# Output product of a gated-merge decoder block: seven half-size products instead of eight, with sums on GpSimd

## The chip, the cores and the metric

The kernel runs on one core of one Trainium2 chip. The time is that of one execution on the device, in microseconds. Three executions of the kernel before took 1394.12, 1395.01 and 1397.86 us; the median is 1395.01. One more execution was recorded by the hardware profiler and is the source of the profile.

A core has five engines with instruction streams of their own: TensorE (PE in the profile; its weight loads are PEld), VectorE (DVE), ScalarE (ACT), GpSimd (POOL) and SyncE (SP), which here only issues DMAs. They meet at semaphores.

## The reference

One layer of a decoder trunk on x of 1024 tokens by 1024 channels, all in float32. A modulated RMS norm gives `h`; `h @ w_in` feeds a gMLP mixer (`y_a`) and a Mamba-2 SSD mixer (`y_b`); two gates merge them; an output product, a residual and a last norm follow:

```python
merged = jax.nn.sigmoid(g_a) * (y_a @ w_proj_a) + jax.nn.sigmoid(g_b) * (y_b @ w_proj_b)
x = x + gate[:, None, :] * (merged @ w_out)
...
return rms_norm(x, final_norm_w)
```

The change concerns `merged @ w_out`, a product of 1024x1024 by 1024x1024, and what surrounds it.

## The kernel before

**Precision.** Every float32 operand of a big product is split in two: a high part (an ACT copy into the type float32r) and a low part (DVE subtracts the high part from the original). A product is then three matmuls: high by high, high by low, low by high.

**Seven products.** The big products before the output product already go by Winograd's variant of Strassen: both operands are cut in quarters, and seven products p1 to p7 of sums of quarters take the place of eight. With quarters a11, a12, a21, a22 and b11 to b22 they are p1 = a11 b11, p2 = a12 b21, p3 = s4 b22, p4 = a22 t4, p5 = s1 t1, p6 = s2 t2, p7 = s3 t3, with sums s1 = a21 + a22, s2 = s1 - a11, s3 = a11 - a21, s4 = a12 - s2 on one side and t1 to t4 on the other.

**Stages.** First come the products of `h` with `w_in` (pairs of column blocks, `pair`, lines 718 to 774), their convolutions and gates (`conv_done` and its neighbours, from 1007). They share six buffers of 128x1024, handed out by `wide` (176). `later` (506) puts off a function by a number of slots, one slot per product of 12 matmuls; `gate_part2` (909) puts off eight calls of `gated_weights` (919), each of which loads 128 rows of `w_out`, multiplies them on POOL by the gate row and stores them. Weights of the merge are prepared there too (`wb_quarter`, 948). Then follow the SSD chunks, with the product for `y_a` between them, and then the branch product `y_b @ w_proj_b` as seven products in the order p1, p2, p5, p3, p6, p7, p4 (1612), eight units of 12 matmuls each; `ahead` (1727) loads seven units ahead and makes operands four units ahead. As a quarter of the branch product is complete, `merged` (1711) adds the other branch to it under its gate and splits the sum in high and low parts. The quarters come in the order (channels 0 to 511, tokens 0 to 511), (channels 0 to 511, tokens 512 to 1023), (channels 512 to 1023, tokens 512 to 1023), and last (channels 512 to 1023, tokens 0 to 511), which are a11, a21, a22 and a12 of the output product.

**The output product** (1835 to 1926) is a plain one. `wo_load` and `wo_parts` bring and split the gated weights, in part during the last branch products. The first two row tiles are multiplied together, k by k; then six row tiles of 128 tokens follow, each 2 halves x 8 k x 3 matmuls of 128x512 (`out_product`, 1868). Behind each row tile DVE adds x, ACT squares and sums, DVE takes the inverse root in nine small operations (`inv_root`, 1857), DVE multiplies by root and norm weight, and the row leaves by SP. The last row is cut in pieces of 512, 256 and 256 columns.

**Order.** Matmuls and loads (line 100) keep the order in which the program has them (`pin`). From the last gate pair to the end of the branch product, `hand[0]` (44 to 58, 1447, 1836) does the same for DVE, ACT and POOL; elsewhere a scheduler may put their instructions in another order when the program is built. SP issues all loads and ACT the stores, each in order: a load that waits for its buffer holds the loads behind it. Buffers of 128x512 are handed out from the list `room` by `slot_tile` (1577) and returned by `give`, the longest free first.

Of the kernel before, what the change touches and what calls it, by code (L numbers as in the profile page):

```python
# [35 lines left out]
def hybrid_kernel(  # L36
# [30 lines left out]
    def dt_(shape, name):  # L67
        return dram.tile(shape, F32, name=name, tag=name)
# [8 lines left out]
    wo_d = [dt_([P, D], f"wo_d{k}") for k in range(KT)]  # L77
# [26 lines left out]
    def store(dst, src):  # L104
        A.dma_start(dst, src)
# [400 lines left out]
    def later(delay, f, *a):  # L506
        tasks.append((slot[0] + delay, f, a))
# [401 lines left out]
    def gate_part2(gb):  # L909
        for n in range(2):  # L910
            pg = bank(f"pg{n}")
            ns = slice(n * 512, (n + 1) * 512)
            mm(pg, ones, gacc[0][:, ns])
            V.tensor_add(gb[:, ns], pg, gb[:, ns])
        V.tensor_scalar_mul(gb, gb, 0.5)
        for k in range(KT):
            later(7 + 11 * k, gated_weights, gb, k)

    def gated_weights(gb, k):

        w = wide(f"wog{k}")
        load(w, w_out[k * P : (k + 1) * P, :])
        G.tensor_mul(w, w, gb)  # L923
        store(wo_d[k], w)


    WB = {"p5": 0, "p7": 1, "p6": 2, "p3": 3, "p4": 4}
# [763 lines left out]
            load(ma, mt_d[b][:, hs])  # L1691
        gates[b, h] = th, ma

    mhl = {}
    places = []

    def m_slot(name):
        if m_sl:
            if not places:
                pool, b = m_sl.pop(0)  # L1700
                t = pool.tile([P, 3, 512], F32R, name=f"m{name}", tag="sl", bufs=b)
                places.extend(t[:, i] for i in range(3))
            return places.pop(0)
        return places.pop(0) if places else slot_tile(name, F32R)

    m_sl = [(p2r, 2), (p2q, 3), (p2q, 3), (p2q, 3), (p2r, 2)]


    GATES = {"p5": (0, 0), "p6": (0, 1), "p7": (4, 1), "p4": (4, 0)}

    def merged(b, h, c, name):

        th, ma = gates.pop((b, h))
        V.scalar_tensor_tensor(th, th, 1.0, c, op0=ALU.add, op1=ALU.mult)
        V.tensor_add(th, th, ma)
# [5 lines left out]
        A.copy(hi, th)  # L1721
        V.tensor_sub(lo, th, f32(hi))
        mhl[b, h] = hi, lo

    LEAD, LOAD = 4, 7

# [38 lines left out]
    wo, wor = {}, {}  # L1765
    KO = (4, 5, 6, 7, 0, 1, 2, 3)

    def wo_load(k):
        wor[k] = [[slot_tile(f"wo{v}{k}_{c}", F32R) for v in "hl"] for c in range(2)]
        for c in range(2):  # L1770
            load(f32(wor[k][c][1]), wo_d[k][:, c * 512 : (c + 1) * 512])

    def wo_parts(k):
        for hi, lo in wor[k]:
            A.copy(hi, f32(lo))
            V.tensor_sub(lo, f32(lo), f32(hi))
        wo[k] = wor.pop(k)

    at_unit = {}
    for i, g in enumerate(groups[NG - 2:]):  # L1780
# [26 lines left out]
    for u, (nm, k) in enumerate(units):  # L1807
        if k == 0:
            if nm == "p1":
                psy = banks("yp2", "y")  # L1810
                psx = banks("x", "x")
            elif nm == "p5":
                psy = banks(f"y{nm}", "y")
            elif nm == "p6":
                room.extend(rb_r[0])
            ps = psy if nm in ("p2", "p5", "p3") else psx
        multiply(u, ps)
        for f in at_unit.get(u, ()):
# [7 lines left out]
        if nm in ("p7", "p4") and k % 2 == 0:  # L1826
            n = k // 2 + (4 if nm == "p4" else 0)
            due_m = 2 * (16 - len(mhl)) - len(places) - 3 * len(m_sl)
            if len(room) >= 4 + due_m and len(wor) + len(wo) < KT:
                wo_load(KO[len(wor) + len(wo)])  # L1830
        if nm == "p4" and k % 2 and wor:
            wo_parts(next(iter(wor)))
# [5 lines left out]
    for n in KO:  # L1838
        if n not in wo:
            if n not in wor:  # L1840
                wo_load(n)
            wo_parts(n)
    ps3.__exit__(None, None, None)


    ps4 = ctx.enter_context(tc.tile_pool(name="ps4", bufs=1, space=PSUM, reuse_waits="tile"))

    for n in range(4):
        ps4.tile([P, 512], F32, name=f"one{n}_0", tag="one", bufs=4)

    def pj_tile(name):
        return ps4.tile([P, 1024], F32, name=name, tag="pj", bufs=2)

    def one(name):
        return ps4.tile([P, 512], F32, name=name, tag="one", bufs=4)

    def inv_root(sq):

        y, t, v = sq[:, 2:3], sq[:, 3:4], sq[:, 1:2]
        V.tensor_scalar(t, sq[:, 0:1], 1.0 / D, EPS, op0=ALU.mult, op1=ALU.add)  # L1860
        V.tensor_scalar(y.bitcast(I32), t.bitcast(I32), -0.5, float(0x5F3759DF), op0=ALU.mult, op1=ALU.add)
        V.tensor_scalar_mul(v, t, -0.5)
# [3 lines left out]
        return y  # L1866

    def out_product(ps, t, k, c, cs):

        tsl = slice(t % 4 * P, (t % 4 + 1) * P)  # L1870
        for a, b in ((0, 0), (0, 1), (1, 0)):
            mm(ps, mhl[k, t // 4][a][:, tsl], wo[k][c][b][:, cs], k == KO[0] and a + b == 0, k == KO[-1] and a == 1)

    xrs = {}

    def ask_x(t):
        xrs[t] = p2q.tile([P, S], F32, name=f"xr{t}", tag="dcy", bufs=3)
        load(xrs[t], x[t * P : (t + 1) * P, :])

    tiles = [4, 5, 6, 7, 0, 1, 2, 3]  # L1880
    ask_x(4)
    ask_x(5)
    fnw = p2r.tile([P, D], F32, name="fnw", tag="w4", bufs=4)
    load(fnw, final_norm_w.unsqueeze(0).to_broadcast([P, D]))
    pws = {t: pj_tile(f"po{t}") for t in tiles[:2]}
    for k in KO:
        for t in tiles[:2]:
            for h in range(2):
                out_product(pws[t][:, h * 512 : (h + 1) * 512], t, k, h, slice(0, 512))

    for n, t in enumerate(tiles):
        tsl = slice(t * P, (t + 1) * P)
        xr = xrs.pop(t)
        if n + 2 < NCH:
            ask_x(tiles[n + 2])
        r = p2r.tile([P, S], F32, name=f"r{t}", tag="dcy", bufs=2)
        sq = dthq[:, 4 * n : 4 * n + 4]
        last = n == NCH - 1
        if last:
            py = [one(f"po{t}_{h}") for h in range(3)]  # L1900
            pieces = [(py[0], 0, 512), (py[1][:, 0:256], 512, 256), (py[2][:, 0:256], 768, 256)]
            part = dde[:, 0:4]
        else:
            pw = pws[t] if n < 2 else pj_tile(f"po{t}")
            pieces = [(pw[:, h * 512 : (h + 1) * 512], h * 512, 512) for h in range(2)]
        for m, (ps, c0, w) in enumerate(pieces):
            cs = slice(c0, c0 + w)
            for k in KO if n > 1 else ():
                out_product(ps, t, k, c0 // 512, slice(c0 % 512, c0 % 512 + w))
            if last:  # L1910
                V.tensor_add(r[:, cs], ps, xr[:, cs])
                A.activation(xr[:, cs], r[:, cs], AF.Square, accum_out=part[:, m : m + 1])  # L1912
                G.tensor_mul(r[:, cs], r[:, cs], fnw[:, cs])  # L1913
        if last:
            V.scalar_tensor_tensor(sq[:, 0:1], part[:, 0:1], part[:, 1:2], part[:, 2:3], op0=ALU.add, op1=ALU.add)
            y = inv_root(sq)
            V.tensor_scalar_mul(r[:, 0:512], r[:, 0:512], y)
            nc.sync.dma_start(out[tsl, 0:512], r[:, 0:512])
            A.mul(r[:, 512:1024], r[:, 512:1024], y)
            nc.scalar.dma_start(out[tsl, 512:1024], r[:, 512:1024])  # L1920
        else:
            V.tensor_add(r, pw, xr)
            A.activation(xr, r, AF.Square, accum_out=sq[:, 0:1])  # L1923
            y = inv_root(sq)
            V.scalar_tensor_tensor(r, r, y, fnw, op0=ALU.mult, op1=ALU.mult)
            nc.sync.dma_start(out[tsl, :], r)
    p2qpool.__exit__(None, None, None)
    p2xpool.__exit__(None, None, None)
    p2rpool.__exit__(None, None, None)
# [30 lines left out]
```

## Time and profile before

| | us |
|---|---|
| median of three executions | 1395.01 |
| lowest, highest | 1394.12, 1397.86 |
| the profiled execution | 1396.63 |
| its span in the profile | 1394.9 |

The span reaches from the first to the last recorded instruction or transfer, so 1.73 us of the profiled execution lie outside it. A row of a group of instructions gives the line (often that of a helper), engine, operation, tiles written and read, shapes and count, then busy time and the mean of one in ns, then the engine's idle time before them and what ended it. A row in order of time gives start and duration in us. A row of stages gives a stretch and its length, then the busy time of each engine with its count of instructions, the granted TensorE clock, the DMA share and GB/s.

### The profile page before, as it was taken

How to read it: one execution, taken by the hardware profiler on the slowest of the kernel's cores; microseconds unless marked ns; L12 is line 12 of the kernel's file. 1: busy time of each engine (PE TensorE's matmuls, PEld its weight loads, DVE VectorE, ACT ScalarE, POOL GpSimd, SP SyncE). 2: the span in 40 equal slices, each digit the busy share in tenths (PEclk: the TensorE clock that was granted, in tenths of full speed). 3: DMA queues.
4: the chain of work that ended last, by engine and by line, in shares of the span. 5: the costliest groups of instructions: out<-in, count | busy, mean ns of one | idle time of the engine just before them, and what ended most of it. 6: DMA issues, size and time to landing. Idle time of an engine off the chain costs nothing.

```text
span 1394.9 us, 20349 instructions
## 1 busy us (share of the span) xinstructions
PE 1370.1 (98%) x7015; PEld 1131.3 (81%) x7015; DVE 1032.8 (74%) x1771; ACT 771.2 (55%) x1420; POOL 211.5 (15%) x198
## 2 busy tenths in 40 slices
PE   8999999999999999999999999999999999999997
PEld 6678888888888888888888788888888878888886
DVE  4666766776677789878988877577888768787743
ACT  6664456566556666555656555577777724233301
POOL 0000000000000000000000010018888860000000
PEclk9999999999999999999999999999999999999999
DMA  8565533333322567677667876598899859987332
GB/s 265 154 223 160 176 110 112 108 99 111 117 91 91 158 183 210 208 245 241 207 207 219 253 226 178 179 333 294 290 316 293 261 148 294 411 263 273 136 121 76
DMA packets 268907, 280.28 MB, mean 201 GB/s; under 512 B 18396, under 2 KB 215428, under 8 KB 268804
## 3 DMA queue, kind: packets, MB, share of 16 engines
q1 hardware_dynamic: 193796, 211.20, 48.3%
q10 hardware_dynamic: 75008, 67.78, 14.3%
q8 instruction: 55, 0.90, 0.3%
q14 instruction: 48, 0.39, 0.1%
HBM read 195.63 MB, written 83.30 MB: 200 GB/s over the span
## 4 chain that ended last, share of the span: by engine, by line
PE 86%; DMA 4%; DVE 3%; ACT 2%; issue 2%; POOL 1%; SPq 1%; POOLq 0%; DVEq 0%; ACTq 0%
PE xx L591 6%; PE xuz L591 6%; PE xcb L591 6%; PE po L91 6%; PE xz L591 6%; PE xg L591 5%; PE x L1680 5%; PE pma L91 4%; PE yp L1680 3%; PE yuz L591 3%; PE ycb L591 3%; PE yx L591 3%; PE vx L703 3%; PE yz L591 3%; PE yg L591 3%; PE vy L703 2%
## 5 line engine op out<-in xcount | busy, mean ns | idle before, releaser
L923 POOL TENSOR_TENSOR wog<-wog,gb 128x1024 f32<-128x1024 f32 x8 | 22.6, 2830 | 647.1 <-DMA wbr<-in_w_proj_b_dram 450.0
L56 ACT ACTIVATE dcy<-dcy,nacs 128x128 f32<-128x128 f32 x256 | 78.3, 388 | 16.9 <-POOL dcy L56 16.4
L56 POOL TENSOR_SCALAR_AFFINE_SELECT dcy<-dcy 128x1024 f32<-128x1024 f32 x32 | 36.4, 1138 | 102.1 <-DVE yh L56 61.3
L91 PE MATMUL pma<-yh,wah 128*128 128x512 f32 x128 | 42.9, 416 | 0.0
L91 PE MATMUL pma<-yh,wal 128*128 128x512 f32 x128 | 42.6, 414 | 0.0
L56 ACT ACTIVATE ea<-dcy 64x512 f32<-64x512 f32 x64 | 40.3, 629 | 4.0 <-DMA dcy<-acs_d 3.5
L56 POOL TENSOR_TENSOR yz<-y,sl 128x512 f32<-128x512 f32 x32 | 41.3, 1290 | 0.6
L56 DVE TENSOR_TENSOR dcy<-dcy,pc 128x1024 f32<-128x1024 f32 x32 | 39.0, 1218 | 2.7 <-PE pc L94 1.8
L1014 ACT ACTIVATE ac<-ac 128x1024 f32<-128x1024 f32 x32 | 34.0, 1061 | 12.6 <-DVE ac L1012 12.4
L56 DVE TENSOR_TENSOR ym<-yn,ea 128x512 f32<-128x512 f32 (+1 forms) x32 | 19.9, 621 | 27.8 <-PE yn L91 27.7
L91 PE MATMUL pma<-yl,wah 128*128 128x512 f32 x128 | 39.9, 393 | 0.0
L56 POOL TENSOR_TENSOR y<-y,ym 128x512 f32<-128x512 f32 (+1 forms) x32 | 36.6, 1143 | 15.3 <-DVE ym L56 15.0
L91 PE MATMUL yi<-dcy,xd 128*64 128x128 f32 x512 | 35.0, 279 | 2.8 <-DVE xe L56 2.5
L1923 ACT ACTIVATE xr<-r 128x1024 f32<-128x1024 f32 x7 | 7.4, 1061 | 53.0 <-issue 39.0
L1012 DVE SCALAR_TENSOR_TENSOR ac<-c2x,cwt,ac 128x1023 f32<-128x1023 f32 (+2 forms) x24 | 30.7, 1280 | 7.7 <-ACT ac L1010 7.6
L1913 POOL TENSOR_TENSOR r<-r,fnw 128x256 f32<-128x256 f32 (+1 forms) x3 | 2.7, 915 | 219.0 <-ACT xr L1912 219.0
L1012 DVE SCALAR_TENSOR_TENSOR ac<-c2cb,cwt,ac 128x1023 f32<-128x1023 f32 (+2 forms) x24 | 30.7, 1281 | 6.1 <-ACT ac L1010 6.0
L91 PEld LDWEIGHTS yi<-dcy,xd 128*64 128x64 f32 x512 | 27.3, 136 | 9.1 <-issue 3.8
L56 DVE SCALAR_TENSOR_TENSOR yn<-yn,par,rb 128x512 f32<-128x512 f32 x32 | 24.4, 762 | 13.6 <-DMA yn<-yb_d 12.3
L91 PE MATMUL sp<-xe,bn 128*128 128x256 f32 x112 | 32.7, 409 | 0.0
L1012 DVE SCALAR_TENSOR_TENSOR ac<-c1cb,cwt,ac 128x1023 f32<-128x1023 f32 (+2 forms) x24 | 30.7, 1280 | 0.8 <-issue 0.8
L1012 DVE SCALAR_TENSOR_TENSOR ac<-c1x,cwt,ac 128x1023 f32<-128x1023 f32 (+2 forms) x24 | 30.7, 1281 | 0.0
(2837 smaller groups left out, 4370.2 us busy)
## 6 DMA issues: line engine op xcount, KB each, us to landing
sl<-s_d SPq DMA_DIRECT2D x32, 768.0 KB
s_d<-ac ACTq DMA_DIRECT2D x32, 512.0 KB
dcy<-acs_d SPq DMA_DIRECT2D x32, 512.0 KB
aw<-in_ada_w_dram SPq DMA_DIRECT2D x16, 512.0 KB
vp<-in_w_in_dram SPq DMA_DIRECT2D x32, 256.0 KB
wbr<-in_w_proj_b_dram SPq DMA_DIRECT2D x64, 128.0 KB
wb_d<-wbb ACTq DMA_DIRECT2D x32, 256.0 KB
wb_d<-wbc ACTq DMA_DIRECT2D x32, 256.0 KB
```

Source lines behind the costliest of these rows:

```text
L56: return lambda *a, **k: tc.keep_in_program_order(f(*a, **k))
L91: pin(PE.matmul(acc, l, r, start=first, stop=last))
L591: pin(PE.matmul(ps, lw[:, k * P : (k + 1) * P], r[k], start=first and n + k == 0, stop=n == 2 and k == 3, skip_group_check=not first))
L703: pin(PE.matmul(ps[j], l[k][:, js], r, start=first and k + m == 0, stop=k == 3 and m == 2, skip_group_check=not first))
L923: G.tensor_mul(w, w, gb)
L1012: V.scalar_tensor_tensor(ac[:, s:], cc[:, : S - s], conv_wt[:, 3 - s, i : i + 1], ac[:, s:], op0=ALU.mult, op1=ALU.add)
L1014: A.activation(ac, ac, AF.Silu)
L1680: pin(PE.matmul(ps[j], a[:, v, js], r, start=first and n + k == 0, stop=n == 2 and k == KT - 1, skip_group_check=not first))
L1913: G.tensor_mul(r[:, cs], r[:, cs], fnw[:, cs])
L1923: A.activation(xr, r, AF.Square, accum_out=sq[:, 0:1])
```

## The change

The output product now goes by the same seven products, in the order p1, p5, p6, p7, p4, p3, p2, so that only the last two need a12, the quarter of the branch product that is done last.

- `gated_weights` is called four times instead of eight and takes two blocks of 128 rows at a time; two slots later `gated_sums` forms four sums on POOL. All seven operands of a row block are stored (seven of 128x512, where two blocks were four).
- In `merged`, quarters go into place as operands; the sums s3, s1 and s2 are formed on POOL, s4 on POOL during p5. `half_sum` splits s3 and s1 between the branch units, or right after them.
- Weights are loaded and split in 28 units of 128x512: eight split and four more loaded during the branch products, the rest during the output product, loads one or two products ahead and splits one product ahead.
- Each product is 4 banks x 4 k x 3 matmuls of 128x512. p1, p6, p7, p4 and p2 use one set of four banks, p5 and p3 the other. p6, p7 and p4 add onto what stands in the bank, and p3 onto p5.
- After each bank its part of the output rows is copied or added (`after_bank`), and the next operands are made (`beside_bank`). x is added on POOL, except to the left half of rows 4 to 7, where DVE adds it with the bank of p4.
- Rows 4 to 7 are complete after p4, and leave during p3 and p2. Rows 0 to 2 leave after their bank of p2, the last row in pieces of 256 columns. Inverse roots are a power on POOL, except that of the last row, which stays on DVE.

The diff, cut to its core:

```diff
-        for k in range(KT):
-            later(7 + 11 * k, gated_weights, gb, k)
+        for k in range(4):
+            later((4, 48, 61, 74)[k], gated_weights, gb, k)
...
-        w = wide(f"wog{k}")
-        load(w, w_out[k * P : (k + 1) * P, :])
-        G.tensor_mul(w, w, gb)
-        store(wo_d[k], w)
+        a, b = (wide(f"wog{i}") for i in (k, k + 4))
+        for t, i in ((a, k), (b, k + 4)):
+            load(t, w_out[i * P : (i + 1) * P, :])
+            G.tensor_mul(t, t, gb)
+        store(wo_d[k][:, 0], a[:, 0:512])
+        store(wo_d[k][:, 5:7], b.rearrange("p (n c) -> p n c", n=2))
+        later(2, gated_sums, a, b, k)
+
+    def gated_sums(a, b, k):
+        b11, b12, b21, b22 = a[:, 0:512], a[:, 512:1024], b[:, 0:512], b[:, 512:1024]
+        G.tensor_sub(b11, b12, b11)
+        G.tensor_sub(b12, b22, b12)
+        G.tensor_sub(b22, b22, b11)
+        G.tensor_sub(b21, b21, b22)
+        for n, t in ((1, a), (3, b)):
+            store(wo_d[k][:, n : n + 2], t.rearrange("p (n c) -> p n c", n=2))
...
-        hi, lo = m_slot(f"mh{b}_{h}"), m_slot(f"ml{b}_{h}")
...
+        if b < 4 and h == 0:
+            m_parts("a11", b, t)
+        elif b < 4:
+            G.tensor_sub(raw[b, 0], raw[b, 0], t)
+            half_sums.append(("s3", b))
+        elif h:
+            m_parts("a22", b - 4, th)
+            G.tensor_add(raw[b - 4, 1], raw[b - 4, 1], th)
+            G.tensor_sub(raw[b - 4, 0], th, raw[b - 4, 0])
+            half_sums.append(("s1", b - 4))
+        else:
+            raw[b, 0] = th
...
+        if nm == "p6":
+            wo_load(k) if k < 4 else wo_parts(k - 4)
+        elif nm == "p7" and k % 2 == 0:
+            wo_load(4 + k // 2)
+        elif nm == "p4":
+            if k % 2 == 0:
+                wo_parts(4 + k // 2)
+            if k > 3:
+                wo_load(4 + k)
...
+    def multiplied(ps, nm, j, cs, w):
+        a, first = mop[OUT[nm][1]], nm in ("p1", "p5", "p2")
+        for k in range(4):
+            for n, (v, r) in enumerate(((0, 0), (0, 1), (1, 0))):
+                pin(PE.matmul(ps, a[k][v][:, j * P : (j + 1) * P], wop[nm, k][r][:, cs], start=first and n + k == 0,
+                              stop=n == 2 and k == 3, skip_group_check=not first))
...
+    def after_bank(nm, j, ps):
+        if nm == "p1":
+            row_tile(j)
+            A.copy(rows[j][:, LEFT], ps)
...
+        elif nm == "p3":
+            r = rows[j][:, RIGHT]
+            V.tensor_add(r, r, ps)
+            square(j, RIGHT, sqr[:, j : j + 1])
+            G.tensor_mul(r, r, fnw[:, RIGHT])
+        elif j < 3:
+            r = rows[j][:, LEFT]
+            V.tensor_add(r, r, ps)
+            square(j, LEFT, sql[:, j : j + 1])
+            roots_of(slice(j, j + 1))
+            V.scalar_tensor_tensor(r, r, root[:, j : j + 1], fnw[:, LEFT], op0=ALU.mult, op1=ALU.mult)
+            A.mul(rows[j][:, RIGHT], rows[j][:, RIGHT], root[:, j : j + 1])
+            out_leave(j, slice(0, D), nc.sync)
...
+    def beside_bank(nm, j):
+        n = OORDER.index(nm)
+        if 0 < n < 5:
+            wo_load(8 + 4 * n + j)
+        if nm == "p5":
+            m_parts("s2", j, raw[j, 0])
+            wo_parts(8 + j)
+            m_parts("a12", j, raw[4 + j, 0])
+            G.tensor_sub(raw[j, 0], raw[4 + j, 0], raw[j, 0])
+            ask_x(4 + j, RIGHT)
...
+        elif nm == "p3":
+            add_x(j, LEFT)
+            wo_parts(24 + j)
...
+    for nm in OORDER:
+        ps, m = out_banks[OUT[nm][0]], OUT[nm][1]
...
+            multiplied(ps[j], nm, j, slice(0, 512), 512)
+            after_bank(nm, j, ps[j])
+            beside_bank(nm, j)
+        if nm != "p2":
+            release_m(m)
+            release_w(nm)
+        if nm == "p4":
+            variance(slice(4, 8))
+            roots_of(slice(4, 8))
+            for t in range(4, 8):
+                V.scalar_tensor_tensor(rows[t], rows[t], root[:, t : t + 1], fnw, op0=ALU.mult, op1=ALU.mult)
+                out_leave(t, slice(0, D), nc.sync)
```

More of the change, by code (lines that the diff above doesn't have):

```diff
@@ L76, in hybrid_kernel @@
     yb_d = [dt_([P, S], f"yb_d{n}") for n in range(2 * NG)]
-    wo_d = [dt_([P, D], f"wo_d{k}") for k in range(KT)]
+    wo_d = [dt_([P, 7, 512], f"wo_d{k}") for k in range(4)]
     th_d = dt_([2 * D, S], "th_d")
@@ L1692, in gate_load, with m_parts @@
         gates[b, h] = th, ma
-    mhl = {}
+    raw, half_sums = {}, []
+    mop = {nm: {} for nm in ("a11", "s3", "a22", "s1", "s2", "s4", "a12")}
     places = []
+    place_of = {}
     def m_slot(name):
[L1698 to L1704, printed above, removed]
+        if m_sl and not places:
+            pool, b = m_sl.pop(0)
+            t = pool.tile([P, 3, 512], F32R, name=f"m{name}", tag="sl", bufs=b)
+            places.extend(t[:, i] for i in range(3))
+        if places:
+            place_of[name] = places.pop(0)
+            return place_of[name]
+        return slot_tile(name, F32R)
     m_sl = [(p2r, 2), (p2q, 3), (p2q, 3), (p2q, 3), (p2r, 2)]
     GATES = {"p5": (0, 0), "p6": (0, 1), "p7": (4, 1), "p4": (4, 0)}
+    def m_parts(nm, k, t):
+        mop[nm][k] = hi, lo = m_slot(f"{nm}h{k}"), m_slot(f"{nm}l{k}")
+        A.copy(hi, t)
+        V.tensor_sub(lo, t, f32(hi))
     def merged(b, h, c, name):
@@ L1825, in hybrid_kernel @@
             gate_load(GATES[nm][0] + k // 2, GATES[nm][1])
[L1826 to L1832, printed above, removed]
+        if half_sums and k % 2 == 0:
+            half_sum(*half_sums.pop(0))
         if due:
             merged(*due)
+        if nm == "p6":
[7 more added lines that the diff above has]
+                wo_load(4 + k)
     emptied_banks("p4")
@@ L1837, in hybrid_kernel @@
     room.extend(bh_r[0] + bl_r[0])
[L1838 to L1862, printed above, removed]
+    while half_sums:
+        half_sum(*half_sums.pop(0))
+    out_banks = {"u": banks("ou", "y"), "w": banks("ow", "x")}
+    OUT = {"p1": ("u", "a11"), "p5": ("w", "s1"), "p6": ("u", "s2"), "p7": ("u", "s3"), "p4": ("u", "a22"),
+           "p3": ("w", "s4"), "p2": ("u", "a12")}
@@ new lines, in hybrid_kernel, with ask_x, add_x, row_tile @@
+    LEFT, RIGHT = slice(0, 512), slice(512, 1024)
+    rows, xr = {}, {}
+    junk = slot_tile("junk")
+    sqr, sql, var, root = (dthq[:, 8 * n : 8 * n + 8] for n in range(4))
+    def ask_x(t, half):
+        xr[t, half.start] = r = gate_slot(f"xr{t}_{half.start}")
+        load(r, x[t * P : (t + 1) * P, half])
+    def add_x(t, half):
+        G.tensor_add(rows[t][:, half], rows[t][:, half], xr.pop((t, half.start)))
+    def row_tile(t):
+        n = len(rows)
+        pool, tag, b = (p2r, "w4", 4) if n < 4 else (p2r, "dcy", 2) if n < 6 else (p2q, "dcy", 3)
+        rows[t] = pool.tile([P, S], F32, name=f"r{t}", tag=tag, bufs=b)
@@ new lines, in square, with release_m, release_w @@
+    def square(t, part, acc):
+        A.activation(junk[:, 0 : part.stop - part.start], rows[t][:, part], AF.Square, accum_out=acc)
+    def release_m(nm):
+        for k in range(4):
+            for v in "hl":
+                t = f"{nm}{v}{k}"
+                if t in tags_of:
+                    give(t)
+                else:
+                    places.append(place_of.pop(t))
+    def release_w(nm):
+        for k in range(4):
+            give(f"woh{nm}{k}")
+            give(f"wol{nm}{k}")
@@ L1865, in inv_root @@
             V.scalar_tensor_tensor(y, t, 1.5, y, op0=ALU.add, op1=ALU.mult)
[L1866 to L1883, printed above, removed]
-    load(fnw, final_norm_w.unsqueeze(0).to_broadcast([P, D]))
[L1885 to L1926, printed above, removed]
```

98 lines of the change are left out of this document (83 added, 15 removed).

## Prediction, made before the changed kernel had run

> **What bounds the kernel now.** I read the first part of the page first (busy shares), then the chain that ended last, then the busy time by stage.
>
> ```profile
> span 1394.9 us, 20349 instructions
> PE 1370.1 (98%) x7015; PEld 1131.3 (81%) x7015; DVE 1032.8 (74%) x1771; ACT 771.2 (55%) x1420; POOL 211.5 (15%) x198
> PEclk9999999999999999999999999999999999999999
> ...
> PE 86%; DMA 4%; DVE 3%; ACT 2%; issue 2%; POOL 1%; SPq 1%; POOLq 0%; DVEq 0%; ACTq 0%
> ```
>
> TensorE (PE) is busy for 98% of the span, at full clock in every slice, and carries 86% of the chain. The page warns that busy matmuls need not be at their peak, so the chain in order of time gives the pace:
>
> ```profile
> 1233.83 43.52 PE x L1680 x192
> 1277.35 22.05 PE x L1680 x96
> 1299.41 84.78 PE po L91 x384
> ```
>
> 192 matmuls of 128x512 in 43.52 us are 0.2267 us each. The output product (po, line 91) starts at 1299.41, right behind the last branch product, and is the chain from there on. By stage, the columns being stretch and length, then PE, PEld, DVE, ACT and POOL busy (with counts), granted clock, DMA share and GB/s:
>
> ```profile
> 600.00:850.00 250.00, 248.21 (x1102) 204.50 (x1102) 212.53 (x393) 145.21 (x252) 22.64 (x8) 1.00 0.73 224
> ...
> 1277.40:1299.40 22.00, 22.00 (x97) 18.20 (x98) 17.88 (x29) 9.99 (x18) 0.00 (x0) 1.00 0.70 258
> 1299.40:1310.30 10.90, 10.90 (x50) 9.03 (x49) 8.54 (x14) 4.42 (x8) 0.00 (x0) 1.00 0.21 66
> ...
> 1321.20:1387.10 65.90, 65.85 (x312) 55.28 (x312) 27.25 (x79) 9.19 (x18) 2.02 (x2) 1.00 0.28 97
> ```
>
> In the output product DVE has 27.25 us of work in 65.90, ACT 9.19, POOL 2: there is room to buy matmuls with vector work. In the branch product before it (1277.40 to 1299.40) DVE is at 17.88 of 22.00; in the stage where the gated output weights are made (600 to 850) it is at 85%.
>
> **The change, part by part.**
>
> *Matmuls.* Before: 8 row tiles x 8 k x 2 halves x 3 = 384 (the last tile's two quarter-width pieces count as one). After: 7 products x 4 banks x 4 k x 3 = 336, same operand shapes. 48 x 0.2267 = **10.9 us less** on PE, and here PE sets the end. That is the only gain.
>
> *Banks.* Four products share the first set of banks (p1, p6, p7, p4), so each bank must be read out before the next product writes it. Between two uses of one bank lie three banks of 12 matmuls, 3 x 12 x 0.2267 = 8.2 us; the copies that read it take 0.6:
>
> ```profile
> L56 DVE TENSOR_TENSOR p6bl<-yn,p6bh 128x512 fp32r<-128x512 f32 x8 | 5.5, 687 | 0.0
> ...
> L1925 DVE SCALAR_TENSOR_TENSOR r<-r,dthq,fnw 128x1024 f32<-128x1024 f32 x7 | 9.0, 1285 | 0.2
> ...
> L56 ACT CAST p6bh<-yn 128x512 fp32r<-128x512 f32 x8 | 5.0, 622 | 5.6 <-DVE yn L56 2.4 <-PE x L1680 1.6 <-PE yp L1680 1.6
> L56 ACT COPY p<-yp 128x512 f32<-128x512 f32 x8 | 4.4, 591 | 0.3
> L1913 POOL TENSOR_TENSOR r<-r,fnw 128x512 f32<-128x512 f32 x1 | 1.3, 1291 | 215.8 <-ACT xr L1912 215.8
> ```
>
> So I cost bank reuse at nothing; the first set is free when the branch products end, and p1's operands (quarter a11 and its weight) are split before, so PE starts p1 without a gap.
>
> *Operands.* Each product needs four k-slices of a branch sum and of a weight sum, each as a high part (ACT cast, 0.62) and a low part (DVE subtract, 0.69). Per product of 10.9 us the heaviest is p5: per bank step it issues a copy, then the parts of s2, of the next weight and of a12, so ACT has 4 x (0.59 + 3 x 0.62) = 9.8 us and DVE 4 x 3 x 0.69 = 8.3. Both fit, barely. The last slice's parts are written behind the copy of the last bank; the next product asks for slice 3 after nine matmuls, 2.0 us. Copy, two casts and two subtracts in strict order are 0.59 + 2 x 0.62 + 2 x 0.69 = 3.2 at worst, so a seam can cost from 0 to 1.2 us. Only matmuls and loads are held to program order here, so these parts may run earlier when their slots are free. Five such seams: 0 to 6; I take **+0.8**, near the low end, because before, the weight parts of this stage were also made this late and PE waited for none of them.
>
> *Weight loads.* 28 loads of 256 KB instead of 16, on SP's queue with the x tiles; issued a product and more ahead, in a stage where DMA is busy for 28% (last row of the stages). Nothing, and 3 us a product if that lead were gone, which I don't expect: a slot is asked for after its last reader is done.
>
> *Sums on POOL.* 16 sums on the weights in the gated stage, 12 in the last branch products, 4 in p5, then 12 additions of x and 4 products with the norm weight. POOL is empty there. The question is what they do to DVE. POOL and DVE side by side are seen where both are busy:
>
> ```profile
> L56 DVE TENSOR_TENSOR dcy<-dcy,pc x29: 1208/1222/1223, 939.6 to 1115.3; 128x1024 f32<-128x1024 f32 x29
> ...
> L56 DVE TENSOR_TENSOR wal<-wa,wah x14: 687/1282/1750, 931.6 to 1119.5; 128x512 fp32r<-128x512 f32 x14
> ```
>
> The numbers are least, median and longest in ns. `wal` reads two SBUF tiles and takes 1.28 us in the median beside POOL, 1.75 at worst, instead of 0.69: **each POOL sum of 1.29 us costs DVE 0.6 to 1.06 us**. `dcy`, with one input in PSUM, does not stretch. The Trainium skill, GPSIMD Engine Reference, section "Key points", says that GpSimd shares its SBUF interfaces with VectorE and contends with DVE instructions with two SBUF inputs; by that rule only these wait, and the two rows agree. Its section "Engine selection" speaks against such sums on GpSimd, as about twice as slow; on DVE a sum would take 0.69, and on POOL it takes 0.6 from DVE anyway.
>
> *Gated stage.* Before it has eight POOL products (wog); one of them shows the whole path to PE:
>
> ```profile
> L923 POOL TENSOR_TENSOR wog<-wog,gb 128x1024 f32<-128x1024 f32 x8 | 22.6, 2830 | 647.1 <-DMA wbr<-in_w_proj_b_dram 450.0 <-DMA wog<-in_w_out_dram 125.9 <-DVE wbr L958 30.9
> ```
>
> ```profile
> 779.78 3.09 POOL L923 TENSOR_TENSOR wog<-wog,gb 128x1024 f32<-128x1024 f32 x1 [31.47 <-DMA wog<-in_w_out_dram]
> ...
> 781.13 2.29 DVE L537 TENSOR_TENSOR p2z5l<-a12z,p2z5h 128x512 fp32r<-128x512 f32 x1
> ...
> 788.28 0.68 DVE L728 TENSOR_TENSOR c2g<-p5g,xg 128x512 f32<-128x512 f32 x1
> ...
> 789.01 1.20 PE L591 MATMUL xg<-t4h,p4g10h 128*128 128x512 f32 x4 [1.79 <-DVE c2g L728]
> ```
>
> A subtract that should take 0.69 took 2.29, until POOL let go; DVE was 1.6 late, the read-out of bank xg came late, and PE stood for 1.79 us, its whole idle time in 600 to 850 (248.21 of 250). Eight such losses are 12.8 us of DVE; 1.79, or 14%, reached PE. After, there are four bursts of two wog and four sums: 4 x (2 x 1.6 + 4 x 0.6) = 22.4 us of DVE (29.8 with 1.06 a sum); 14% is 3.1, less the 1.8 of before: **+1.3 us**, with ends at -1.8 (no burst meets a tight place) and +20.6 (all of it reaches PE).
>
> *Last branch products, p1 and p5.* DVE: at most the 17.9 us of before in the branch product p4 (a sum's part stands where a weight's part stood), 9 x 0.69 = 6.2 in p1 (four merges of two operations, one part), 8.3 in p5: 32.4 in 22.0 + 2 x 10.9 = 43.8 us. 12 POOL sums add 7 to 13, or 15.5 if DVE waited for all of 1.29: 40 to 48. The operands of the branch products are made four units ahead. I take 0; the upper end is 47.9 - 43.8 = +4.1.
>
> *Rows 4 to 7 leave in p3.* DVE in p3: 4 additions, 4 weight parts and 4 products of 1.285 = 10.6 us in 10.9, beside 8 POOL sums, which add 4.8 to 10.3. DVE ends p3 4.5 to 10 us late unless the weight parts ran earlier; p2 asks it for two operations of 0.69 and a small one per row, some 6 of 10.9, so 0 to 5.1 us are still late at the end. I take **+0.5**, near the low end, as p2's weights can be split in p4.
>
> *The tail.* The same chain as before, less one small operation; row 2's root now passes over POOL:
>
> ```profile
> 1387.09 0.42 DVE L1911 TENSOR_TENSOR r<-po,xr 128x256 f32<-128x256 f32 x1 [2.45 <-PE po L91]
> ...
> 1388.09 0.78 DVE L1915 SCALAR_TENSOR_TENSOR dthq<-dde 128x1 f32<-128x1 f32 x1 [0.58 <-ACT xr L1912]
> ...
> 1391.48 0.37 ACTq L1920 DMA_DIRECT2D out_dram<-r  x1
> ```
>
> From the last addition to the last store it is 4.4 us. I take no change, within 0.5 either way.
>
> **Sum.** -10.9 + 0.8 + 1.3 + 0.5 = -8.3 us. Against the profiled execution: span 1394.9 to 1386.6, its time 1396.63 to 1388.3. That execution lies 1.62 above the median of the three runs, 1395.01, so the median goes to **1386.7 us**.
>
> **Rivals.**
> 1. *Output stage bound by DVE.* POOL's sums and the finishing of rows 4 to 7 hold DVE at the upper ends above: +4.1 before p6 and +5.1 at the end instead of +0.5. 1386.7 + 4.1 + 4.6 = **1395.4**; halfway, 1391. For it: p3's 10.6 of 10.9 before any contention. Against it: parts may move ahead, and DVE is idle for over half of the stage before.
> 2. *Slower: the weight bursts stop PE in the gated stage.* Mechanism: POOL holds DVE, DVE reads a bank out late, PE waits, as at 789.01. If all 22.4 us reach PE: 1386.7 - 1.3 + 20.6 = **1406.0**. It ends above the time of before from 11.4 us of PE idle there (1.8 + 10.9, less 0.8 + 0.5 for seams and p3), half of DVE's loss. For it: 85% busy DVE, longer bursts, two wide buffers of six held at once. Against it: 14% was the share for eight losses at eight places.
> 3. *Nothing lost:* the bursts miss tight places and the seams close: -10.9 - 1.8 = **1382.3**.
> 4. *It doesn't do what it says:* rows 4 to 7 leave only behind p2. Then up to 5.1 us of DVE stand at the end as in 1; I count it there.
>
> **How the numbers follow.** Forecast (1384 to 1389.5) 0.62; nothing lost 0.07; rival 1 (1389.5 to 1396) 0.18; rival 2 0.13. About 0.3%, 4.2 us, is what a measurement tells from no change: the bounds are 1390.8 and 1399.2. Faster: 0.62 + 0.07 + a third of rival 1 = 0.75; same: 0.12 + 0.03 of rival 2 = 0.15; slower 0.10. Range 1383.5 to 1394.0: about 0.05 lies below, 0.05 of rival 1 and rival 2's 0.13 above; the ends of the seams and of p3 lie inside.
>
> **What would show it.** 48 matmuls fewer, and the output product 76 us long (336 x 0.2267) with idle PE of under 2 us in it; seams show as PE waits for a low part at a product's first bank. In 600 to 850 PE idle of some 3 us behind POOL's sums, with DVE subtracts of 1.3 to 2.3 us. In p3 the 128x1024 products of rows 4 to 7 stretched past 1.285. Last addition to last store near 4.4. It is wrong if PE waits for a DMA in the output stage, for a wide buffer in the gated stage, or if the branch products before p1 stall.

## The result, and the profile after

The changed kernel takes 1408.03 us in the median of seven executions (1401.59 to 1412.28), the kernel before 1395.23 beside it (1393.75 to 1399.0, seven). The ratio is 1.0079, with a 95% interval of 1.0056 to 1.0103: it is slower by 12.8 us, where 8.3 less had been forecast. The profiled execution of after is the longest of the seven, 1412.28 us, so its readings lie 4.2 us above the median.

The first part of the page of after, and its chain:

```profile
span 1410.6 us, 20411 instructions
PE 1367.4 (97%) x6955; PEld 1125.1 (80%) x6955; DVE 1075.5 (76%) x1745; ACT 793.8 (56%) x1473; POOL 290.1 (21%) x249
...
PE 75%; DVE 9%; DMA 6%; issue 4%; ACT 3%; POOL 2%; SPq 1%; ACTq 0%; DVEq 0%; POOLq 0%
```

PE's share of the chain fell from 86% to 75%, and DVE's rose from 3% to 9%. To find the place, take landmarks that both kernels have: the products for `y_a` (pma) and the last matmul. Of before, then of after (the numbers behind the colon are least, median and longest in ns, then first and last start in us):

```profile
L91 PE MATMUL pma<-yh,wah x128: 387/393/583, 921.9 to 1143.9; 128*128 128x512 f32 x128
...
1386.77 0.28 PE L91 MATMUL po<-woh,mmh 128*128 128x256 f32 x1
```

```profile
L91 PE MATMUL pma<-yh,wah x128: 387/393/586, 940.0 to 1165.5; 128*128 128x512 f32 x128
...
1320.59 2.73 PE ou L1944 x12
...
1402.48 0.28 PE L1944 MATMUL olast<-wohp,a12l 128*128 128x256 f32 x1
```

| stretch | before | after | difference |
|---|---|---|---|
| start to first pma | 921.9 | 940.0 | +18.1 |
| first pma to last pma | 222.0 | 225.5 | +3.5 |
| last pma to the output product | 155.5 | 155.1 | -0.4 |
| output product to end of last matmul | 87.6 | 82.2 | -5.5 |
| last matmul to end of span | 7.8 | 7.8 | 0 |

The sum is +15.7, the difference of the two spans. The output product did get shorter, by half of what was expected; three times as much was lost 400 us ahead of it, where the weights are gated. The same stage as in the prediction's table, of after, and two stretches of it:

```profile
600.00:850.00 250.00, 235.50 (x1022) 190.93 (x1020) 216.50 (x366) 132.74 (x231) 48.55 (x24) 0.99 0.72 222
...
755.00:765.00 10.00, 7.98 (x28) 6.45 (x29) 5.59 (x9) 4.50 (x9) 0.98 (x2) 0.83 0.61 193
...
758.00:761.00 3.00, 3.00 (x9) 2.33 (x8) 0.77 (x2) 0.58 (x1) 0.00 (x0) 0.50 0.59 155
```

1022 matmuls instead of 1102: 80 x 0.2267 = 18.1 us, the whole of the first row of the table. PE is idle for 14.5 us instead of 1.79, and for some microseconds its clock is lower (0.50 in the last row; the last section comes back to it). A stand is from here on a time in which PE waits. What ended the stands (engine and tile, what it waited for, us in total, times, longest), from 590 to 930 us:

```profile
PE xcb L591 <- DVE c2cb L728: 3.0, 2, 2.2
PE xz L591 <- DVE c2z L728: 2.6, 2, 2.3
PE xg L591 <- DVE c2g L728: 2.3, 1, 2.3
PE ycb L591 <- ACT p5cb L728: 2.0, 1, 2.0
PE xz L591 <- ACT c1z L728: 1.9, 1, 1.9
PE xx L591 <- DVE c2x L728: 1.8, 1, 1.8
PE xg L591 <- ACT c1g L728: 1.1, 1, 1.1
```

All seven rows are readouts of PE's banks that came late (line 728), most of them on DVE. Not every stand has a GpSimd operation beside it. The one behind `c2x` and the one of 1.10 behind `c1g`, 2.9 us of the 14.7, lie at 672.91 and 706.37, and POOL did nothing from 628.4 to 747.64 (the 119.29 in its row further down):

```profile
672.91 1.19 PE L591 MATMUL xx<-t4h,p4x5h 128*128 128x512 f32 x4 [1.84 <-DVE c2x L728]
```

What makes these two is not shown; run e11 below, which has no GpSimd products in this stage, stands at the same matmul for 1.20 us. One of the others in order of time, POOL, DVE and PE:

```profile
747.64 7.59 POOL L924 TENSOR_TENSOR wog<-wog,gb 128x1024 f32<-128x1024 f32 x2 [119.29 <-PE xz L591]
```

```profile
750.06 0.69 DVE L728 TENSOR_TENSOR c1z<-c1z,zz 128x512 f32<-128x512 f32 x1
750.66 2.32 DVE L537 TENSOR_TENSOR p7x6l<-a21x,p7x6h 128x512 fp32r<-128x512 f32 x1
752.90 2.87 DVE L537 TENSOR_TENSOR p4x6l<-a22x,p4x6h 128x512 fp32r<-128x512 f32 x1
...
756.30 0.67 DVE L728 TENSOR_TENSOR c2z<-p5z,xz 128x512 f32<-128x512 f32 x1
```

```profile
757.02 1.59 PE L591 MATMUL xz<-t4h,p4z4h 128*128 128x512 f32 x4 [2.29 <-DVE c2z L728]
```

Two subtracts take 2.32 and 2.87 us instead of 0.69 each, beside POOL's two products. Whatever is queued behind them is 3.8 us late (5.19 less two times 0.69), and that is the readout `c2z`, for which PE waits. A readout that DVE does beside POOL, with one input in PSUM, is not slowed: `c1z`, at 750.06, took 0.69.

With the sums one sees how the two engines take turns; POOL first, then DVE:

```profile
765.63 1.28 POOL L932 TENSOR_TENSOR wog<-wog,wog 128x512 f32<-128x512 f32 x1
766.99 1.82 POOL L933 TENSOR_TENSOR wog<-wog,wog 128x512 f32<-128x512 f32 x1
768.89 1.29 POOL L934 TENSOR_TENSOR wog<-wog 128x512 f32<-128x512 f32 x1
```

```profile
765.73 1.33 DVE L969 TENSOR_TENSOR wbr<-wbr 128x128 f32<-128x128 f32 x1
766.99 0.68 DVE L537 TENSOR_TENSOR p3g10l<-s4g,p3g10h 128x512 fp32r<-128x512 f32 x1
767.59 1.37 DVE L970 TENSOR_TENSOR wbr<-wbr 128x128 f32<-128x128 f32 x1
768.99 1.33 DVE L971 TENSOR_TENSOR wbr<-wbr 128x128 f32<-128x128 f32 x1
770.36 0.29 DVE L972 TENSOR_TENSOR wbr<-wbr 128x128 f32<-128x128 f32 x1
```

The first sum of 128x128 on DVE takes 1.33, until POOL's is done, and not 0.29 as the last one, which has no POOL sum beside it. Then DVE's subtract comes first and takes 0.68, and POOL's sum is the one that is stretched, to 1.82; the next DVE sum waits for it. In these rows each operation with two SBUF inputs waits for the whole rest of the other engine's.

What DVE lost in all can be read from its busy time up to the first pma. Before and after have the same 1170 DVE operations there; run e12 below, which has no GpSimd products in this stage, has these and one more. Before, after, e12:

```profile
0.00:921.90 921.90, 911.78 (x4276) 750.67 (x4276) 693.39 (x1170) 544.00 (x899) 29.04 (x21) 1.00 0.57 176
...
0.00:940.00 940.00, 917.08 (x4275) 751.34 (x4276) 712.23 (x1170) 542.33 (x898) 56.00 (x37) 1.00 0.57 176
...
0.00:924.00 924.00, 912.66 (x4276) 749.46 (x4276) 681.03 (x1171) 543.80 (x899) 6.61 (x13) 1.00 0.57 175
```

So DVE lost some 12.4 us to GpSimd before the change and some 31.2 after it: 18.8 more, where PE lost 18.1.

In the output stage one seam stands, between p5 and p6. The stretch of p5 and the one behind it, then POOL, DVE and PE in it:

```profile
1331.50:1347.20 15.70, 11.80 (x52) 9.33 (x51) 15.70 (x19) 9.05 (x18) 10.76 (x6) 1.00 0.10 23
1347.20:1358.10 10.90, 10.89 (x41) 8.82 (x42) 9.82 (x11) 6.22 (x11) 4.01 (x3) 0.84 0.98 344
```

```profile
1336.44 6.83 POOL L1988 TENSOR_TENSOR mr<-tg,mr 128x512 f32<-128x512 f32 x3 [5.50 <-DVE ma11h L1730]
1343.23 3.38 POOL L1900 TENSOR_TENSOR r<-r,xr 128x512 f32<-128x512 f32 x2
```

```profile
1343.74 1.74 DVE L56 TENSOR_TENSOR tg<-tg,tha 128x512 f32<-128x512 f32 x1
1345.41 1.75 DVE L1818 TENSOR_TENSOR wolp<-wolp,wohp 128x512 fp32r<-128x512 f32 x1
```

```profile
1347.21 0.50 PE L1944 MATMUL ou<-wolp,ma11l 128*128 128x512 f32 x1 [3.91 <-DVE wolp L1818]
```

DVE is busy for all of 15.70 us, its operations at 1.7 to 1.8 instead of 0.69 while POOL forms s4 and adds x, and the low part of p6's last weight slice comes 3.9 us late. Then 41 matmuls in 10.9 us where 48 belong, at a granted clock of 0.84: another 1.6 us.

### The profile page after: what moved, and what is told of

The parts are those of the page before. It is cut to its first block, busy times and chain, and to the rows that moved or that the text cites. A ratio compares the mean times of both kernels' runs of the same rounds, so it can differ in the third digit from the quotient of the medians.

```text
span 1410.6 us, 20411 instructions
## 1 busy us (share of the span) xinstructions
PE 1367.4 (97%) x6955; PEld 1125.1 (80%) x6955; DVE 1075.5 (76%) x1745; ACT 793.8 (56%) x1473; POOL 290.1 (21%) x249
## 4 chain that ended last, share of the span: by engine, by line
PE 75%; DVE 9%; DMA 6%; issue 4%; ACT 3%; POOL 2%; SPq 1%; ACTq 0%; DVEq 0%; POOLq 0%
PE x L1692 6%; PE xuz L591 6%; PE xcb L591 5%; PE xx L591 5%; PE yp L1692 5%; PE xz L591 4%; PE xg L591 4%; PE pma L91 4%; PE yuz L591 3%; PE vx L703 3%; PE ou L1944 3%; PE yx L591 3%; PE ycb L591 3%; PE vy L703 2%; PE yz L591 2%
## 5 line engine op out<-in xcount | busy, mean ns | idle before, releaser
L56 DVE SCALAR_TENSOR_TENSOR y<-sl,dskt,yi 128x256 f32<-128x256 f32 x64 | 27.6, 473 | 2.6 <-POOL yz L56 2.6
```

The costliest lines, as they stand in the source:

```text
L56: return lambda *a, **k: tc.keep_in_program_order(f(*a, **k))
```

## The experiments

Theory: GpSimd's work in the gated stage holds VectorE, and nearly all of that reaches PE. Rivals: the output stage is the one that loses; the weights are held too long or stored too late; ScalarE's queue, on which the stores wait for GpSimd, carries the cost.

**Which half of the change loses.** e1 is the changed kernel with the gated stage of before (eight single products, no sums), e2 the kernel before with the gated stage of after.

```diff
 e1
-        for k in range(4):
-            later((4, 48, 61, 74)[k], gated_weights, gb, k)
+        for k in range(KT):
+            later(7 + 11 * k, gated_weights, gb, k)
...
-        later(2, gated_sums, a, b, k)
```

> The changed kernel with the gated stage of before: eight single products on POOL at their old slots, no sums; all seven weight places are written, so the same bytes are stored, but four of them hold plain quarters, so that the weights' sums are left out. Theory 1 (POOL's bursts hold DVE in the gated stage, which costs some 13 us of PE idle and slow clock there, while the output product alone gives some 5.5): about 1389 to 1391. Theory 2 (two wide buffers of six held per burst, so that read-outs wait for a buffer): the same. Theory 3 (the loss comes from elsewhere, a new order of the whole program or the sums in the branch products): stays above 1400.

> The kernel before with the new gated stage alone: pairs of products at the new slots and four sums each on POOL, stored to places that nothing reads; the plain weights are stored too and the old output product reads them. Theories 1 and 2: 1395 plus 12 to 18, some 1407 to 1413. Theory 3: within 3 us of 1395.

Measured: e1 1390.35 (ratio to before 0.9959, interval 0.9944 to 0.9975), e2 1414.96 (1.0144, 1.0123 to 1.0164). The output side alone wins 4.9 us, the gated side alone loses 19.7. The output stage is not where the loss is.

**Sums or products.** e3 is e2 without the sums (`gated_sums` only stores); e4 is the changed kernel with `V.tensor_sub` for its four `G.tensor_sub`.

> As the gated stage alone, but without the four sums: the two wide buffers are held and stored as long, POOL does only the pairs of products. Theory 1: most of the loss goes, 1396 to 1402 (two products back to back still hold DVE). Theory 2: the loss stays, 1406 or more.

> The changed kernel with the four sums of the gated stage on DVE instead of POOL: 16 operations of 0.69 us more on DVE, none of 1.3 to 1.8 on POOL. Theory 1: DVE loses less than beside POOL, and the time falls to 1396 to 1402. Theory 2 (buffers held, whoever sums): it stays at 1405 to 1408.

Measured: e3 1404.33 (1.0069, 1.0052 to 1.0086), e4 1394.33 (0.9997, 0.9983 to 1.0011). The sixteen sums cost 10.6 us from e3 to e2, and 13.7 from e4 to the changed kernel: 0.66 and 0.86 us each. The next runs ask where e3's 9 us come from, which have no sums in them.

**What the pairs cost without sums.** All on the kernel before. e5 loads and holds pairs and stores them twice, without any product (the multiplication by the gate is left out, as in e11, e12 and e15); e6 has pairs of products, not held; e11 is e5 with the second store cut to 16 columns; e12 is e5 without hold and second store; e15 is e11 with the stores on GpSimd's queue.

```diff
 e5
             load(t, w_out[i * P : (i + 1) * P, :])
-            G.tensor_mul(t, t, gb)
...
+        later(2, held_store, a, b, k)
 e11
-            store(wx_d[k][:, n], t)
+            store(wx_d[k][:, n, 0:16], t[:, 0:16])
 e15
-            store(wx_d[k][:, n, 0:16], t[:, 0:16])
+            G.dma_start(wx_d[k][:, n, 0:16], t[:, 0:16])
```

> The kernel before, with the pairs of w_out loaded, held and stored twice as in e3_pairs_no_sums, but without any product on GpSimd: the multiplication of w_out by the gate is left out. Theory T1 (the 9 us of e3 come from two GpSimd products in a row, beside which VectorE's two-input operations stand): 1392 to 1396, at or below the kernel before, the first pma matmul at or before 922. Theory T2 (they come from holding two wide buffers for two slots, so that other loads of w wait): still 1400 to 1405, pma at 927 to 930.

> The kernel before, with two GpSimd products in a row at the slots of the changed kernel, stored once, and no buffer held afterwards. T1 (bursts of two products): 1400 to 1405 as in e3, with waits of PE for VectorE's readouts c2 of 2 to 3 us. T2 (held buffers): 1394 to 1397, as the kernel before.

> e5_hold_only with the second store cut to 16 of 1024 columns: the pairs are held for two slots as there, but 4.1 MB of stores are gone. The multiplication of w_out by the gate is left out here too. If holding two wide buffers is the price of e5 (7.8 us over before): 1401 to 1405. If the second stores are: 1392 to 1397.

> e5_hold_only with no hold and no second store: pairs of w_out are loaded and stored once, and the multiplication by the gate is left out. If hold or second store is the price of e5: 1391 to 1396, at or below before. If the price is the first store, which now waits on ScalarE's queue for the load to land with nothing between: 1400 to 1405 here and in e11 alike.

> e11_hold_small_store (1401.9; no multiplication by the gate) with the stores issued by GpSimd. If its 5.5 us over e12 come from ScalarE standing at a store whose load hasn't landed (3.5 and 3.8 us at 782 and 788 us in its trace): 1393 to 1397. If they come from the two held buffers: 1400 to 1403.

Measured: e5 1403.75 (1.0054, 1.0037 to 1.0071), e6 1398.28 (1.0021, 1.0009 to 1.0034), e11 1401.91 (1.0039, 1.0026 to 1.0053), e12 1396.36 (0.9997, 0.9984 to 1.0009), e15 1402.24 (1.0046, 1.0031 to 1.0060). So in these kernels the hold, with a second store of 16 columns, costs 5.5 us (e11 less e12) and products in pairs about 2.3 (e6), and e5 came out where T2 had it, not T1. The trace of e11 seemed to show how: ScalarE stood for 3.83 us behind a store of a pair.

```profile
787.95 0.33 ACTq L106 DMA_DIRECT2D wx_d<-wog  x1
...
791.49 1.06 ACT L1033 ACTIVATE c1g<-c1g 128x1024 f32<-128x1024 f32 x1 [3.83 <-DMA wx_d<-wog]
```

But e15, whose stores are not on ScalarE's queue, is as slow. What the hold costs through, and why the kernels below hold pairs as long and lose nothing, stays open.

**The second loss.** e7 is e4 with p5 relieved, e8 is e4 with the eight gate products on VectorE too.

```diff
 e7 (p5 in beside_bank)
-            m_parts("a12", j, raw[4 + j, 0])
-            G.tensor_sub(raw[j, 0], raw[4 + j, 0], raw[j, 0])
-            ask_x(4 + j, RIGHT)
+            if j == 3:
+                hand[0] = True
+                for i in range(4):
+                    m_parts("a12", i, raw[4 + i, 0])
+                    V.tensor_sub(raw[i, 0], raw[4 + i, 0], raw[i, 0])
+                hand[0] = False
...
 e8
-            G.tensor_mul(t, t, gb)
+            V.tensor_mul(t, t, gb)
```

> e4_sums_on_dve with product p5 relieved: VectorE makes the weight parts first, the parts of a12 and the differences s4 come behind the parts of its last pass and on VectorE, and x is asked for and added one product later. If the seam between p5 and p6 stands because GpSimd's s4 and x sums stretch VectorE's operations ahead of the last weight part: the wait of 3.9 us for the weight part is under 1 us and the time 1387 to 1391, 3 to 6 us under e4. If VectorE's sum of work in p5 is what binds, whoever runs beside it: the wait stays at 3 to 4 us or moves to the next seam, and the time is 1393 to 1396.

> e4_sums_on_dve with the eight gate products on VectorE as well, so that GpSimd does nothing in the gated stage. T1 (GpSimd's bursts are the price): 1388 to 1393, below e4, pma at 921 to 924. T2 (held buffers): 1394 as e4, pma at 925 or later. If VectorE has no room for 8 more products of 128x1024 (about 1.1 us each): above 1397.

Measured: e7 1389.29 (0.9960, 0.9947 to 0.9973), e8 1391.61 (0.9976, 0.9964 to 0.9988): 5.0 and 2.7 us under e4. The wait at the seam, of e7:

```profile
PE ou L1944 <- DVE wolp L1818: 0.3, 1, 0.3
```

3.9 us became 0.3. e7 moves sums from GpSimd, makes the weight parts first and adds x a product later; which of these did it was not told apart.

**Burst, queue or contention.** e10 is the changed kernel with the four sums of a pair in four slots; e13 is the changed kernel with the stores of w_out issued by GpSimd.

```diff
 e10
-        G.tensor_sub(b12, b22, b12)
-        G.tensor_sub(b22, b22, b11)
-        G.tensor_sub(b21, b21, b22)
+        later(1, G.tensor_sub, b12, b22, b12)
+        later(2, G.tensor_sub, b22, b22, b11)
+        later(3, gated_last, a, b, k)
 e13 (and both other stores of gated weights)
-        store(wo_d[k][:, 0], a[:, 0:512])
+        G.dma_start(wo_d[k][:, 0], a[:, 0:512])
```

> The changed kernel with the four GpSimd sums of each pair in four slots, one in each, instead of four in a row. If a burst is what hurts, because VectorE loses several waits in a row and PE's banks run out: most of the 13.7 us that the sums cost (changed kernel less e4_sums_on_dve) comes back, 1394 to 1400. If each sum costs VectorE the same wherever it stands: 1405 to 1410, as the changed kernel.

> The changed kernel with the stores of w_out (first and second) issued by GpSimd itself instead of ScalarE. If ScalarE standing behind those stores carries the cost to PE: most of the 17.7 us between the changed kernel and e1_old_gated_stage comes back, 1391 to 1399, and ScalarE's gaps of 4 to 7 us ahead of its readouts at 615, 625, 790 and 805 us are gone. If VectorE being held by GpSimd's operations is the price: 1403 to 1409, PE's waits for the c2 sums of VectorE stay.

Measured: e10 1406.41 (1.0060, 1.0040 to 1.0081), e13 1409.74 (1.0078, 1.0053 to 1.0103). Neither helps: each sum costs its price wherever it stands, and ScalarE's queue doesn't carry it.

**Both mended.** e9 is e8 with e7's p5; e14 is e9 with the stores of w_out issued by GpSimd, as in e13.

> e8_gated_on_dve with the relieved p5 of e7_p5_lighter: nothing on GpSimd in the gated stage, and the weight parts of p5 made first. If the two prices are independent: e8 (1391.6) less the 5.0 us that e7 gained over e4, so 1385 to 1388, no wait of PE for a weight part over 1 us. If they share a cause (VectorE short of room everywhere): 1389 to 1392.

> e9_both_mended with the stores of w_out issued by GpSimd. In e9's trace PE's waits in the gated stage are 2 us in all, so at most that can be won: 1383 to 1386. If issuing stores on GpSimd costs VectorE something: above 1387.

Measured: e9 1385.28 (0.9910, 0.9895 to 0.9925), e14 1383.54 (0.9904, 0.9881 to 0.9926; before 1395.71 beside it). e14 beats both kernels, the one before by 12.2 us. The gated stage and the output product of e14:

```profile
600.00:850.00 250.00, 250.00 (x1112) 206.32 (x1111) 220.66 (x423) 149.41 (x255) 8.82 (x16) 1.00 0.78 240
```

```profile
1298.13 10.88 PE ou L1944 x48
...
1374.18 0.28 PE L1944 MATMUL olast<-wohp,a12l 128*128 128x256 f32 x1
```

PE is never idle in the 250 us, though DVE has more work of its own than in either kernel, 220.66 us. From 1298.13 to 1374.46 the output product takes 76.3 us; 336 x 0.2267 is 76.2.

**Contention by itself.** e16 adds to e14 four GpSimd products by ones beside the sums of each pair, on which nothing waits for long; e17 adds copies in their place.

```diff
 e16
+        later(2, spare_ops, gb[:, 0:512])
+
+    def spare_ops(t):
+        v = t.rearrange("p (n c) -> p n c", n=4)
+        for _ in range(4):
+            G.tensor_mul(v, v, ones.unsqueeze(1).to_broadcast([P, 4, P]))
 e17
+            G.tensor_copy(t, t)
```

> e14_best_stores_off_act with four GpSimd products of 128x512 by ones (two inputs in SBUF) beside the sums of each pair, sixteen in all, at the slots where the changed kernel has its GpSimd sums; nothing waits for them but the next pair's products, a hundred microseconds later. If GpSimd holds VectorE: 16 times the 0.76 us that each sum cost between e4 and e10, so 1393 to 1397. If the lateness of the sums was the price and not contention: 1383 to 1386.

> As e16, with sixteen copies of 128x512 (one input in SBUF) instead of the products. If any GpSimd operation on SBUF holds VectorE: 1390 to 1396. If only one with two inputs does: 1383 to 1386.

Measured: e16 1396.68 (1.0004, 0.9989 to 1.0020), e17 1386.10 (0.9923, 0.9899 to 0.9947). Sixteen products that nothing needs cost 13.1 us against e14, 0.82 each; sixteen copies 2.6, 0.16 each, with an interval that overlaps e14's. The gated stage of e16, POOL's products in it, and a DVE subtract beside them; then the same DVE subtract in e14:

```profile
600.00:850.00 250.00, 241.16 (x1052) 196.15 (x1052) 221.95 (x400) 138.06 (x239) 32.54 (x32) 0.99 0.74 229
...
L933 POOL TENSOR_TENSOR gb<-gb,ones 128x512 f32<-128x512 f32 x16 | 23.4, 1465 | 0.9
...
757.65 1.79 DVE L537 TENSOR_TENSOR p6g10l<-s2g,p6g10h 128x512 fp32r<-128x512 f32 x1
```

```profile
752.39 0.69 DVE L537 TENSOR_TENSOR p6g10l<-s2g,p6g10h 128x512 fp32r<-128x512 f32 x1
```

60 matmuls fewer than e14 in the same 250 us: 60 x 0.2267 = 13.6 us, about the loss of time. That is contention alone: hold and stores are those of e14, and nothing waits for the products. Nor is it another order of instructions: from 590 us to the first pma, DVE's 494 instructions of e14 and ScalarE's 332 stand in the same order in e16. DVE's 494 took 12.4 us longer in sum, 0.78 for each product. Of e17, its copies and the subtract ahead of that one, the most stretched of the two:

```profile
L932 POOL COPY gb<-gb 128x512 f32<-128x512 f32 x16 | 13.1, 820 | 0.6
...
752.27 0.91 DVE L537 TENSOR_TENSOR p5g10l<-s1g,p5g10h 128x512 fp32r<-128x512 f32 x1 [2.43 <-ACT p5g10h L536]
```

A copy takes 0.82 us instead of 1.47, and the subtract beside it 0.91 instead of 0.69. The same 494 instructions, again in the same order, took 3.8 us longer than in e14.

## Why the prediction was wrong

**The failed step** is the share in the gated stage: "14% is 3.1, less the 1.8 of before: +1.3 us, with ends at -1.8 (no burst meets a tight place) and +20.6 (all of it reaches PE)". It measured +18.1 in the trace, near the upper end. Two things in it were off.

The first is the time that DVE loses. For the eight products before, 12.8 was right (12.4 by the busy times above). For the changed stage 22.4 was forecast, 29.8 with the upper price of a sum, and 31.2 was measured. Single stretches of 1.04 (0.29 to 1.33) and 1.10 (0.69 to 1.79) lie at the upper price, 1.06, but the forecast was added up with the lower, 0.6. From e3 to e2 sixteen sums add some 16 us to DVE's busy time up to the first pma, from e4 (less its own sums, 16 x 0.69) to the changed kernel some 20: 1.0 to 1.3 for each.

The second is the share. Of the 18.8 us that DVE lost more than before, PE lost 18.1, and not 14%. The 14% came from one wait behind eight products. e12, which has none of them (and loads w_out in pairs), is no faster than the kernel before (0.9997): the first 12.4 us of DVE cost nothing that can be measured. From e14 to e16, 12.4 us of DVE cost 13.1. One wait among losses that were nearly all hidden could not be carried over to losses on top of them.

In time, the changed kernel less e1 is 17.7 us: sums 13.7 (to e4), products on GpSimd 2.7 (e4 to e8), 1.3 left (e8 to e1). Rival 2 is what happened, its mechanism and its order of size (1406.0); at 0.13 it was given too little. That it came so near has luck in it: the stage lost 18.1 where it had 20.6, from 31.2 us of DVE instead of 22.4, and the output product won less. Of what spoke for it, 85% busy DVE does not decide: in e14 DVE is busy for 88% with work of its own and PE loses nothing. Why work that DVE has of its own passes free, while time taken from it by GpSimd arrives at PE, the runs do not say. e16 shows the second for one order of instructions, that of e14; whether another order would hide it was not tried.

The Trainium skill, GPSIMD Engine Reference, section "Key points", has GpSimd contend with DVE instructions with two SBUF inputs: the trace agrees: beside POOL's products 0.69 for `c1z`, with one input in PSUM, and 2.32 for the subtract of the same size behind it. Its section "Engine selection" asks how long an operation lasts on GpSimd and names about twice VectorE's time for two inputs; here 1.29 to 1.82 against 0.69. What decided is the time taken from DVE: 1.0 to 1.3 us for a sum that DVE would have done in 0.69. The prediction had the two numbers to compare, 0.69 and 0.6 to 1.06, and compared with the lower.

**Matmuls**, -10.9: right; 76.3 us in e14.

**Seams**, +0.8: five seams were counted, four cost nothing, one 3.9 and a slower clock behind it 1.6. It is the one that the upper end of "last branch products, p1 and p5" foresaw (+4.1, where 0 was taken): DVE reached p6 late.

**Rows 4 to 7**, +0.5: their four products took 5.90 us instead of 4 x 1.285 = 5.14, with one POOL product of 1.45 beside them, and PE waited for none of it.

```profile
1384.29 5.90 DVE L2039 SCALAR_TENSOR_TENSOR r<-r,dthq,fnw 128x1024 f32<-128x1024 f32 x4
```

**Tail**, 0: right, 7.8 us both times. **First to last pma**, 0 by silence: +3.5 in the trace of after, but not a lasting part of the change: in the traces of e10 and e13, with the same work in the gated stage, the stretch is 221.7 and 221.9 us, as before (222.0).

Together the output product won 5.5 us instead of 9.6, and the stage before it lost 18.1 instead of 1.3.

## What to carry to other kernels

Where VectorE reads PE's banks, an operation on GpSimd with two SBUF inputs is not free work on an idle engine: price it as VectorE time of up to its own length (here 0.8 to 1.3 us for operations of 1.3 to 1.8), and compare that with doing it on VectorE. A share of losses that were hidden at a few places says nothing about more losses elsewhere; when its ends are -1.8 and +20.6, the forecast hangs on that term, and not on the -10.9 that is certain. To learn what such a term is worth, add the suspected operations where nothing needs them: here sixteen idle products cost 13.1 us, where the sixteen sums had cost 13.7.

## What the runs showed of the hardware that was not expected

After some of PE's stands the granted clock is low for some microseconds: 0.83 in the mean from 755 to 765 us, and 0.50 from 758 to 761, behind a stand of 2.29 us (28 matmuls in 7.98 us of busy time, where 35 belong), 0.84 in the mean behind the 3.91 of the seam. The stand of 1.79 in the kernel before is followed by four matmuls in 1.20 us, the one of 2.29 by four in 1.59 and the next four in 1.91:

```profile
758.41 1.91 PE L591 MATMUL xz<-t4l,p4z4h 128*128 128x512 f32 x4
```

So a stand of PE can cost more than its length. Length alone does not decide: in the same trace the clock fell behind a stand of 2.00 us, at 828.32, and not behind one of 2.35:

```profile
799.34 1.20 PE L591 MATMUL xg<-t4h,p4g10h 128*128 128x512 f32 x4 [2.35 <-DVE c2g L728]
```

The Trainium skill, TensorE: Matmul & The Clock Gate, section "Why this matters for your kernels", asks for no gap over about 3 us; 2.00 and 2.29 were enough here. And the hold goes both ways: POOL's own products of 128x1024 took from 2391 to 4790 ns in the changed kernel.

```profile
L924 POOL TENSOR_TENSOR wog<-wog,gb x8: 2391/2833/4790, 613.5 to 823.3; 128x1024 f32<-128x1024 f32 x8
```
